# Four raw-weight buffers and five split pairs in place of six and four, with pieces split four ahead

## The chip, the cores and the metric

The kernel runs on one core of one Trainium2 chip. The metric is device time in microseconds (us) of one launch. The engines are named as in the profile: PE is TensorE (PEld its weight loads), DVE is VectorE, ACT is ScalarE, POOL is GpSimd, and SP is SyncE, which here only issues transfers; its queue is written SPq.

## The reference, cut to what matters

One layer of a hybrid decoder block for 256 tokens of width 2048, in float32. Cut down:

```
hn = rms_norm(x, ln_gain)
z  = hn @ w_in + b_in                 # one wide projection, 2048 rows of weights
y_a = rglru(z.lru_x) * silu(z.lru_gate)
y_b = nsa(z.nsa_q, z.k/v ...) * silu(z.nsa_gate)     # compressed, selected, window attention
y_c = fox(z.fox_q, z.fox_k, z.fox_v, z.fox_f) * silu(z.fox_gate)
merged = sum over b of sigmoid(z.merge[b]) * (y[b] @ w_branch[b])
h   = x + merged @ w_out
out = h + sigmoid(h @ w_ple_gate) * rms_norm(p @ w_ple)
```

Nearly all the work is a row of 256 tokens times a great deal of weights, each weight used once.

## The kernel before, in words

**Pieces.** All weights stream through the core once, in the order of their use, as pieces of at most 128 partitions by 1024 float32 (512 KB). There are 384 of them, in the list `halves` that `plan()` makes. A usual piece is two slices of 128 weight rows by 512 columns. Products are made to nearly float32 accuracy out of three cheaper ones: every operand is split into a rounded high part and the remainder, its low part, and PE adds high*high, high*low and low*high (`mm3`). A usual piece is 12 matmuls of 512 columns. In one stretch every fourth piece belongs to the compression of the attention branch (`cmp`); it costs PE only eight short matmuls, though its load and its split are as large as any other.

**The life of a piece.** SP loads it into a buffer `raw` (`issue`). ACT rounds it into the tile `wh`, and DVE subtracts to make `wl` (`cut`). PE then multiplies with both. A load into a raw buffer has to wait until DVE and ACT have read the piece that lay in it; a split into a pair `wh`, `wl` has to wait until PE has finished the piece that lay in that pair. The constants set how many buffers there are and where in the program each step stands:

```
RAW, LOADS, AHEAD = 6, 7, 3
h["raw"] = wp.tile([P, 1024], F32, tag="raw", bufs=RAW, ...)
h["whl"] = [wp.tile([P, 1024], R32, tag=x, bufs=AHEAD + 1, ...) for x in ("wh", "wl")]
for i, h in enumerate(halves):
    while issued <= i + (4 if i < EARLY else LOADS) ...: issue(halves[issued])
    while ready <= i + (2 if i < EARLY else AHEAD) ...: prepare(ready)      # splits the piece
    ... the products of piece i, then side work
```

So, before, the load of piece j waits for the split of piece j-6, and the split of piece j waits for the products of piece j-4. For the first ten pieces (`EARLY`) the program splits only two ahead.

**Side work.** The three mixers, the norms, gates and turns of layout are generators, run a step at a time between pieces by `Side.tick`. Their small products go to four PSUM tiles `bank0` to `bank3`, in between the main products, whose tiles are called `main`. Names that begin with `k_` are side tiles. A turn of layout (`cross`) is a transpose on DVE, four transfers on the SP queue behind whatever loads stand there, and a later read. How much side work goes where is decided while the program is built, by a planner (`Clock`, `Side`) that keeps an estimated time for PE, DVE, ACT and the others: side work stops when DVE or ACT is over a limit ahead of PE (`LIMITS`, 2.5 to 3.5 us), and a small product is put in a margin (`MARGIN`, 1.6 us) after the estimated end of what it reads. The planner knows nothing of the number of buffers. Each engine then runs its own instructions strictly in that order.

Of the kernel before, what the change touches and what calls it, by code (L numbers as in the profile page):

```python
# [1387 lines left out]

RAW, LOADS, AHEAD = 6, 7, 3

FINE = 3
EARLY = 10
# [85 lines left out]
```

## Time and profile before

| | us |
|---|---|
| median of 3 runs | 1060.82 (1060.35 to 1060.99) |
| profiled execution | 1061.77 |
| its span on the core | 1060.0 |
| PE busy | 1053.3 |
| DVE busy | 772.2 |
| ACT busy | 620.6 |

The span runs from the first to the last instruction; the profiled execution's own time is 1.77 us more, which lies around it. Busy PE says little by itself, since matmuls overlap and their ends are modelled. What matters is whether PE waits, and for which engine.

### The profile page before, as it was taken

Reading aid. Unit: us, or ns where it says so; the run is one execution under the profiler, and the core shown is the slowest. Engines: PE = TensorE matmul, PEld = TensorE weight load, DVE = VectorE, ACT = ScalarE, POOL = GpSimd, SP = SyncE. Lnnn points to the kernel's source line nnn. Section 1 sums busy time; section 2 is a strip of 40 time slices with the busy share of each in tenths; the row PEclk is TensorE's granted clock in tenths of the full one; section 3 lists DMA queues with packets and bytes.
Section 4 is the critical chain, followed back from the end, with each engine's and each line's share of the span. In section 5 each row is a group of like instructions: output and inputs, shape, how many; then the busy total and the mean of one; then the engine's idle time right before and its main releaser. Section 6 shows DMA issues by size and latency. Waiting matters only on the chain.

```text
span 1060.0 us, 14061 instructions
## 1 busy us (share of the span) xinstructions
PE 1053.3 (99%) x4903; PEld 879.3 (83%) x4903; DVE 772.2 (73%) x1151; ACT 620.6 (59%) x940; POOL 53.1 (5%) x77
## 2 busy tenths in 40 slices
PE   9999999999999999999999999999999999999998
PEld 7888889888888888888888888888888888888886
DVE  7777889897778678678987965555766566766664
ACT  7668877768766667544645644555555444444442
POOL 0000001110000000020110000000001000000000
PEclk9999999999999999999999999999999999999999
DMA  9767868787657467577677566766676877778751
GB/s 337 248 201 260 257 200 280 233 266 226 217 189 218 150 198 216 182 234 251 194 235 239 186 222 207 223 213 214 219 244 196 264 235 220 236 250 257 278 207 60
DMA packets 86295, 237.52 MB, mean 224 GB/s; under 512 B 14024, under 2 KB 31312, under 8 KB 86224
## 3 DMA queue, kind: packets, MB, share of 16 engines
q1 hardware_dynamic: 81504, 220.87, 64.8%
q0 software_dynamic: 4720, 15.76, 5.5%
q8 instruction: 38, 0.62, 0.3%
q14 instruction: 33, 0.27, 0.1%
HBM read 215.61 MB, written 4.20 MB: 207 GB/s over the span
## 4 chain that ended last, share of the span: by engine, by line
PE 91%; DVE 3%; DMA 2%; ACT 2%; SPq 1%; issue 1%; DVEq 0%; ACTq 0%
PE main L208 87%; PE bank L208 4%; SPq L208 1%; DVE wl L208 1%; DMA raw<-in_w 1%; DMA k_fpz<-k_fprob 1%; DMA k_pz<-k_prob 1%; ACT wh L208 0%; ACT k_pz L208 0%; DVE k_fq L208 0%; DVE k_prob L208 0%; DVE k_fprob L208 0%; DVE k_pt L208 0%; DVE k_fbias L208 0%; DVE k_fx L208 0%
## 5 line engine op out<-in xcount | busy, mean ns | idle before, releaser
L208 DVE TENSOR_TENSOR wl<-raw,wh 128x1024 fp32r<-128x1024 f32 (+2 forms) x388 | 459.8, 1197 | 186.0 <-ACT wh L208 185.2
L208 ACT ACTIVATE wh<-raw 128x1024 fp32r<-128x1024 f32 (+2 forms) x388 | 400.2, 1040 | 318.3 <-PE main L208 281.3
L208 PE MATMUL main<-wh,k_hnh 128*128 128x512 f32 (+2 forms) x1026 | 395.0, 385 | 0.5 <-ACT wh L208 0.5
L208 PE MATMUL main<-wh,k_hnl 128*128 128x512 f32 (+1 forms) x1024 | 393.0, 384 | 0.0
L208 PE MATMUL main<-wl,k_hnh 128*128 128x512 f32 (+2 forms) x1026 | 392.9, 384 | 0.0
L208 PEld LDWEIGHTS main<-wh,k_hnh 128*128 128x128 f32 x1026 | 193.2, 189 | 37.5 <-ACT wh L208 1.1
L208 PEld LDWEIGHTS main<-wh,k_hnl 128*128 128x128 f32 x1024 | 192.5, 188 | 38.1
L208 PEld LDWEIGHTS main<-wl,k_hnh 128*128 128x128 f32 x1026 | 193.2, 189 | 35.9 <-DVE wl L208 0.2
L208 PE MATMUL main<-wl,k_yh 128*128 128x512 f32 x192 | 74.9, 390 | 0.1
L208 PE MATMUL main<-wh,k_yh 128*128 128x512 f32 x192 | 74.9, 390 | 0.0
L208 PE MATMUL main<-wh,k_yl 128*128 128x512 f32 x192 | 74.8, 389 | 0.0
L208 PE MATMUL main<-wh,k_mth 128*128 128x512 f32 x128 | 49.8, 389 | 0.0
L208 PE MATMUL main<-wl,k_mth 128*128 128x512 f32 x128 | 49.8, 389 | 0.0
L208 PE MATMUL main<-wh,k_mtl 128*128 128x512 f32 x128 | 49.8, 389 | 0.0
L208 PE MATMUL main<-wh,k_hth 128*128 128x512 f32 x128 | 49.8, 389 | 0.0
L208 PE MATMUL main<-wl,k_hth 128*128 128x512 f32 x128 | 49.8, 389 | 0.0
L208 PE MATMUL main<-wh,k_htl 128*128 128x512 f32 x128 | 49.8, 389 | 0.0
L208 PEld LDWEIGHTS main<-wl,k_yh 128*128 128x128 f32 x192 | 36.0, 188 | 7.7 <-DVE wl L208 0.5
L208 PEld LDWEIGHTS main<-wh,k_yl 128*128 128x128 f32 x192 | 36.0, 188 | 7.5
L208 PEld LDWEIGHTS main<-wh,k_yh 128*128 128x128 f32 x192 | 36.1, 188 | 7.4
L208 ACT ACTIVATE k_mg<-k_mg 128x512 f32<-128x512 f32 x24 | 15.2, 633 | 26.6 <-DVE k_mg L208 26.3
L208 PEld LDWEIGHTS main<-wl,k_mth 128*128 128x128 f32 x128 | 24.0, 188 | 5.0
(243 smaller groups left out, 948.4 us busy)
## 6 DMA issues: line engine op xcount, KB each, us to landing
raw<-in_w SPq DMA_DIRECT2D x369, 512.0 KB, 4.5
bias<-in_b_in POOLq DMA_DIRECT2D x21, 256.0 KB, 5.2
raw<-in_w SPq DMA_DIRECT2D x8, 408.0 KB, 4.0
k_pz<-k_prob SPq DMA_DIRECT2D x16, 128.0 KB, 4.2
e_dram<-k_e POOLq DMA_DIRECT2D x4, 512.0 KB, 3.6
k_merged<-k_zt SPq DMA_DIRECT2D x16, 128.0 KB, 3.2
k_xc<-in_x POOLq DMA_DIRECT2D x4, 512.0 KB, 6.4
k_hx<-k_zt SPq DMA_DIRECT2D x16, 128.0 KB, 3.6
```

The costliest lines, as they stand in the source:

```text
L208: r = call(out, *args, **kw)
```

## The change

Raw buffers go from six to four, pairs from four to five, and from piece 10 on the program splits a piece four ahead of its products and not three. In memory the two come out alike: 6 + 2*4 = 14 tiles of 4 KB per partition before, and 4 + 2*5 = 14 after.

```
-RAW, LOADS, AHEAD = 6, 7, 3
+RAW, LOADS, AHEAD = 4, 7, 4
```

Now the load of piece j waits for the split of piece j-4, and the split of piece j for the products of piece j-5. Each engine has as many instructions as before (4892 on PE, 1153 on DVE, 869 on ACT, 568 on SP, 82 on POOL); since the planner adds up other times, some stand elsewhere.

On DVE, where the program changes from two ahead to the larger distance: `wl` tiles are low parts of weight pieces, `k_xacc` is the sum of squares for the first norm, `sp_spl` a softplus. Before:

```order
L208 TENSOR_TENSOR wl_425<-raw_366,wh_424 128x1024
L208 TENSOR_TENSOR wl_429<-raw_391,wh_428 128x1024
L208 TENSOR_TENSOR k_xacc_142<-k_xacc_142,k_sq_432 128x512
L208 TENSOR_TENSOR k_xacc_142<-k_xacc_142 128x256
L208 TENSOR_TENSOR wl_451<-raw_416,wh_450 128x1024
L208 TENSOR_SCALAR sp_spl_306<-sp_spl_305 128x8
```

After, in the same place:

```order
L208 TENSOR_TENSOR wl_425<-raw_366,wh_424 128x1024
L208 TENSOR_TENSOR wl_429<-raw_391,wh_428 128x1024
L208 TENSOR_TENSOR wl_433<-raw_416,wh_432 128x1024
L208 TENSOR_TENSOR k_xacc_142<-k_xacc_142,k_sq_436 128x512
L208 TENSOR_TENSOR wl_454<-raw_418,wh_453 128x1024
L208 TENSOR_TENSOR k_xacc_142<-k_xacc_142 128x256
```

The split of the piece in `raw_416` has moved ahead of the side work, and every later split stands one piece further forward.

On the SP queue, where queries are turned (`k_qn`) some 90 pieces in; `raw` rows are loads of pieces. Before:

```order
L208 DMA raw_2197<-in_w 128x1024
L208 DMA raw_2224<-in_w 128x1024
L208 DMA k_qn_2106<-k_zt_2177 128x1x256 x4
L208 DMA raw_2242<-in_w 128x1024
L208 DMA raw_2266<-in_w 128x1024
```

After:

```order
L208 DMA raw_2207<-in_w 128x1024
L208 DMA raw_2228<-in_w 128x1024
L208 DMA raw_2242<-in_w 128x1024
L208 DMA k_qn_2109<-k_zt_2205 128x1x256 x4
L208 DMA raw_2268<-in_w 128x1024
```

The loads stand in the same order, and the turn stands behind one load more. Most turns keep their place.

On PE, the first products of the sparse attention (`bank` from `kk` and the split queries `k_qh`, `k_ql`). Before, they follow main products of the first merged branch (`k_yh`, `k_yl`):

```order
L208 MATMUL main_83<-wl_2939,k_yh_2768 128x512
L208 MATMUL main_83<-wh_2938,k_yl_2769 128x512
L208 MATMUL bank_87<-kk,k_qh_2753 128x272 x2
L208 MATMUL bank_87<-kk,k_ql_2754 128x272
L208 MATMUL bank_88<-kk,k_qh_2753 128x272 x2
```

After, they follow products of the wide projection (`k_hnh`, `k_hnl`):

```order
L208 MATMUL main_84<-wl_2544,k_hnh_128 128x512
L208 MATMUL main_84<-wh_2543,k_hnl_129 128x512
L208 MATMUL bank_87<-kk,k_qh_2623 128x272 x2
L208 MATMUL bank_87<-kk,k_ql_2624 128x272
L208 MATMUL bank_88<-kk,k_qh_2623 128x272 x2
```

The planner has put this group 16 pieces earlier (at piece 103 and not 119). The other groups of that branch come 0 to 6 pieces earlier, the last one where it was, and all groups of the forgetting attention (`fox`, with `k_fk`, `k_fpt`, `k_fx`) stand at the same pieces as before.

## The prediction

> **What bounds the kernel now.** I read the page first, then the waits of PE, the chain that ended last, and the engines by stage.
>
> ```profile
> PE 1053.3 (99%) x4903; PEld 879.3 (83%) x4903; DVE 772.2 (73%) x1151; ACT 620.6 (59%) x940; POOL 53.1 (5%) x77
> ```
>
> Busy PE could hide stalls, so the waits and the pace must confirm it. All waits of PE in the span:
>
> ```profile
> PE bank L208 <- PEq L1473: 0.8, 1, 0.8
> PE main L208 <- ACT wh L208: 0.5, 1, 0.5
> PE bank L208 <- DVE k_fpt L208: 0.2, 1, 0.2
> ```
>
> The chain that ended last (start, length, what, how many):
>
> ```profile
> 5.39 37.24 PE main L208 x158
> ...
> 107.83 0.93 PE bank L208 x8
> 108.77 8.19 PE main L208 x36
> ...
> 617.00 438.03 PE main L208 x1932
> ```
>
> From 617 us to the tail the chain is PE alone, 1932 matmuls at 226.7 ns; the 36 at 108.77 take 227.5 ns each, in the busiest stretch of side work. So PE runs at one pace nearly throughout and sets the time. By stage (window, its length, then busy PE, PEld, DVE, ACT, POOL, granted clock, DMA share, GB/s):
>
> ```profile
> 60.00:250.00 190.00, 190.00 (x1004) 162.40 (x1003) 163.29 (x241) 143.14 (x219) 12.59 (x14) 1.00 0.75 239
> 250.00:617.00 367.00, 366.53 (x1714) 305.64 (x1713) 287.99 (x550) 228.04 (x412) 21.58 (x31) 1.00 0.68 211
> 617.00:1055.00 438.00, 438.00 (x1933) 362.32 (x1931) 276.85 (x282) 208.35 (x245) 16.27 (x24) 1.00 0.70 220
> ```
>
> DVE is 86% busy from 60 to 250 us (163.29 of 190), 78% to 617 and 63% after.
>
> **First term: splits one piece further ahead.** No instruction is added or removed, so PE's work is unchanged. A stall of PE that the earlier split could remove is needed for a gain. The 0.8 us and the 0.5 us lie in the first 6 us, which the change leaves alone (first four loads, two ahead for ten pieces). The middle window shows 367.00 - 366.53 = 0.47 us idle, the others none. Gain between 0 and 0.47; I take 0.3, since the late split at 371 us (below) is one of its causes and gains a piece.
>
> **Second term: the load waits for the split four pieces back.** With six buffers the load waits for the split six back. One such place, DVE, ACT and SP rows of the stretch (piece numbers from counting: DVE's rows from 108.41 are pieces 40, 41 with 42, and 43; ACT's from 116.33 are 44, 45 with 46, and 47):
>
> ```profile
> 108.41 1.22 DVE L208 TENSOR_TENSOR wl<-raw,wh 128x1024 fp32r<-128x1024 f32 x1
> 111.43 2.35 DVE L208 TENSOR_TENSOR wl<-raw,wh 128x1024 fp32r<-128x1024 f32 x2
> 114.37 1.22 DVE L208 TENSOR_TENSOR wl<-raw,wh 128x1024 fp32r<-128x1024 f32 x1
> ...
> 116.33 1.06 ACT L208 ACTIVATE wh<-raw 128x1024 fp32r<-128x1024 f32 x1
> 118.16 2.01 ACT L208 ACTIVATE wh<-raw 128x1024 fp32r<-128x1024 f32 x2
> 120.66 1.06 ACT L208 ACTIVATE wh<-raw 128x1024 fp32r<-128x1024 f32 x1
> ...
> 109.66 0.33 SPq L208 DMA_DIRECT2D raw<-in_w  x1
> ```
>
> Piece 40's split ends at 109.63 and the load of piece 46 leaves at 109.66: SP does wait for it. After the change the load of 44 waits there. All splits shift by a piece together, so the distances in these rows carry over: from the end of split 40 to ACT's start on 44 is 116.33 - 109.63 = 6.7 us, from 43 to 47 it is 120.66 - 115.59 = 5.1. A load needs this long (loads of pieces from 60 to 250 us, then from 617 on):
>
> ```profile
>   PE main L208: 24.7, 19
> DMA to landing us min/median/max: 2.8/4.6/7.2
> ...
>   PE main L208: 185.4, 119
> DMA to landing us min/median/max: 3.5/4.5/8.3
> ```
>
> With the median 4.6 there remain 0.5 to 2.1 us; with the slowest, 7.2, ACT gets its piece 2.1 us late. Today ACT hardly ever waits for a load:
>
> ```profile
> ACT wh L208 <- DMA raw<-in_w: 2.3, 5, 0.9
> ```
>
> What covers a late load: ACT's own idle time for lack of a pair (24.7 us from 60 to 250, in the fence above), DVE's queue behind ACT, and the piece more of lead. How thin the cover was:
>
> ```profile
> 160.53 1.06 ACT L208 ACTIVATE wh<-raw 128x1024 fp32r<-128x1024 f32 x1 [0.60 <-PE main L208]
> 165.06 2.10 DVE L208 TENSOR_TENSOR wl<-raw,wh 128x1024 fp32r<-128x1024 f32 x2
> 166.50 0.93 PE bank L208 x8
> ```
>
> The first of the two low parts at 165.06 is done near 166.2, and PE multiplies with it from 166.5 at the latest; ACT had finished 3.5 us before DVE began, so there ACT may be 3 us late without loss. The new lead gives DVE one piece more: four pieces, one of them `cmp`, take 108.77 + 8.19 - 107.83 = 9.13 us, 2.3 each. So 2.1 late against 2.3 gained: I take 0.3 us of stalls, from 0 up to the first rival's 7. After 617 us PE holds ACT back 119 times for 185.4 us in all, and a late load only uses that up: nothing. Without that cover the price would be the first rival's.
>
> [...]
>
> **Third term: the SP queue and thin joints.** SP runs in order, so turns of layout stand behind loads that now wait for a newer split, at most one piece (2.7 us at 12 matmuls of 227 ns) longer. SP already waits mostly for splits, and three places have nothing to spare:
>
> ```profile
> SPq L208 <- DVE wl L208: 588.5, 276, 8.4
> ```
>
> ```profile
> 370.67 1.19 DVE wl L208
> 371.91 4.15 PE main L208 x17
> ...
> 395.63 1.16 DVE k_prob L208
> 396.84 0.56 SPq L208
> ...
> 398.76 3.35 DMA k_pz<-k_prob
> 402.13 1.07 ACT k_pt L208
> ...
> 405.80 0.63 PE bank L208 x3
> ...
> 538.59 2.02 DMA k_fpz<-k_fprob
> 540.76 0.53 ACT k_fpt L208
> 541.93 0.80 PE bank L208 x4
> ```
>
> At 371 the split itself was last; it gains a piece. At 402 and 540 ACT reads a turn within 0.2 us of its landing, and PE's small products follow. Before the one at 402, DVE finished its transpose at 396.79 and SP issued at 396.84: SP stood free, so much of the 2.7 us need not show. But the attention between 300 and 430 us is also put in another order, first products 16 pieces earlier, which may thin it or crowd it. Bounds -0.5 (the crowding goes) to +5 (two joints fully late); I take 0.5, near the small end, because the forgetting attention keeps its places.
>
> **The first ten pieces.** The load of piece 4 now waits for the split of piece 0 and so on, while the transfers are at their limit (337 GB/s in the first slice), so a later issue lands about as early: 0.
>
> ```profile
> GB/s 337 248 201 260 257 200 280 233 266 226 217 189 218 150 198 216 182 234 251 194 235 239 186 222 207 223 213 214 219 244 196 264 235 220 236 250 257 278 207 60
> ```
>
> **Sum.** -0.3 + 0.3 + 0.5 + 0 = +0.5 us on the profiled span of 1060.0, which with 1.77 around it makes 1061.77, itself 0.95 above the median. On the median 1060.82 this gives 1061.3: no change that a measurement of this kernel tells from none (0.2%, 2.1 us).
>
> **Rivals.**
>
> *The ring of four loads binds (slower).* One turn of a raw buffer is load 4.6, ACT 1.05, DVE 1.2, together 6.9 us, against 9.27 us that PE needs for four pieces from 60 to 250 us (190 us, 82 splits). If waiting in ACT's and DVE's queues takes more than 2.4 us per turn on average, the ring sets the pace. For it: DVE is 86% busy there and the 3.5 us wait at 161.6 is in the rows. Against it: ACT still has 24.7 us to give. At 3.0 us the loss is 0.6 in each of 20 turns, 12 us, less some 5 of lead at the start: +7, 1068 us.
>
> *The turns come late at the thin joints (slower).* Third term at its upper end, two joints at 2 us or more: 1065. For it the zero slack at 402 and 540; against it SP standing free at 396.84, and the forgetting attention's turns at their old places.
>
> *A stall that lets the clock drop.* The launch shows slow matmuls:
>
> ```profile
> 8.11 0.63 PE L208 MATMUL main<-wl,k_hnh 128*128 128x512 f32 x1
> 8.54 0.63 PE L208 MATMUL main<-wh,k_hnl 128*128 128x512 f32 x1
> ```
>
> They start 0.43 us apart, against 0.227 in the chain later, and this lasts from 5.39 to at least 8.54. If one stall brought that back, it would cost itself (the length of such a slow stretch, 3 us or more) and half of a like stretch after it, 1.6: 1061.3 + 3 + 1.6 = 1066. [...]
>
> *The lead pays (faster).* At most 0.47 us of idle PE can go, under the 2.1 that would be told from no change.
>
> **Chances.** Forecast 0.67; ring 0.18; joints 0.10; clock 0.02; over 0.2% faster 0.03. So faster 0.03, same 0.67, slower 0.30. The range reaches from 1059.8 (0.47 gained and half a us of scatter, as the runs had) to 1067, which takes in the joints, the clock and the milder half of the ring.
>
> **What the next profile would show.** If I am right: PE's waits together stay under 3 us, the chain from about 617 us is PE alone; ACT's waits for loads grow from 2.3 us but stay under some 25, mostly before 250 us; SP's waits for low parts grow from 588.5; ACT's waits for PE shrink before 250 us. If the ring binds, PE waits for `wl` or `wh` many times between 60 and 250 us, and ACT for loads just before. If the joints fail, PE waits a few times for `bank` operands between 300 and 620 us. A wait of PE after 617 us would speak against all of this.

## The result, and the profile after

| | before | after |
|---|---|---|
| median (6 runs each, same chip) | 1061.17 us | 1067.58 us (1065.41 to 1069.2) |
| ratio | | 1.0057 [1.0042, 1.0071] |
| span of the profiled execution | 1060.0 us | 1063.6 us |

The change makes the kernel 0.6% slower. The profiled execution is the fastest of the six and lost 3.6 us, while the median lost 6.4. These are two questions: where 3.6 us went, and what most other runs lost besides. One of the ten runs of e5 below took 1164.15 us at a granted clock of 0.851, and the ratios leave such a run out.

The chain that ended last says when it was lost. Its long last piece is as long as before (438.03 us) and starts 3.75 us later, so all of it is lost before 620 us:

```profile
620.75 438.01 PE main L208 x1932
```

Waits of PE after (engine, what waits, for what: us in total, times, longest):

```profile
PE bank L208 <- DVE k_fpt L208: 2.4, 1, 2.4
PE main L208 <- ACT wh L208: 1.1, 1, 1.1
PE bank L208 <- PEq L1473: 0.8, 1, 0.8
PE bank L208 <- DVE k_wds L208: 0.7, 1, 0.7
PE main L208 <- ACT k_yh L208: 0.6, 1, 0.6
...
```

(Two more are of 0.3 and 0.2 us.) The 1.1 us lies at 7 us and does not show on balance: set side by side, the pieces of the two traces start 0.4 us earlier after the change at piece 12. Luck has a part in that, since the full clock is granted from 4.6 us on in this execution and from 9.2 us on in the one before, where matmuls of 512 columns still start 0.43 us apart at 8.54 and 0.23 us apart from 9.33. By 62 us, with some side work moved, 0.1 us of it is left. The pieces start 0.9 us later after 124 us (`k_wds`, gate weights of the recurrent mixer), 1.5 us later by piece 192, and 3.7 us later after 543 us (`k_fpt`, turned probabilities of the forgetting attention). Two places carry most of it: 0.9 us arise at the first and 2.2 us at the second.

ACT's and SP's waits grew as the steps of the change would have it:

```profile
ACT wh L208 <- DMA raw<-in_w: 56.6, 51, 5.4
ACT wh L208 <- PE main L208: 217.8, 146, 2.4
...
SPq L208 <- DVE wl L208: 654.6, 293, 6.6
```

ACT waits for loads 51 times and not 5, and SP stands for low parts 66 us longer. By stage (columns as in the prediction):

```profile
60.00:250.00 190.00, 189.00 (x1000) 161.34 (x999) 161.53 (x238) 139.98 (x216) 12.01 (x13) 1.00 0.72 234
250.00:617.00 367.00, 363.97 (x1701) 303.45 (x1700) 288.18 (x549) 227.76 (x414) 22.72 (x33) 1.00 0.68 210
```

PE is idle 1.00 us in the first stage (before 0) and 3.03 in the second (before 0.47).

**The place at 543 us.** SP's queue there, before and then after (a row is one kind of transfer, and its length runs from the first to the last of the group):

```profile
533.38 0.33 SPq L208 DMA_DIRECT2D raw<-in_w  x1
533.76 2.51 SPq L208 DMA_DIRECT2D k_fq<-k_zt  x4
536.37 2.81 SPq L208 DMA_DIRECT2D k_fpz<-k_fprob  x4
```

```profile
534.89 2.30 SPq L208 DMA_DIRECT2D raw<-in_w  x2
537.25 2.52 SPq L208 DMA_DIRECT2D k_fq<-k_zt  x4
539.87 2.99 SPq L208 DMA_DIRECT2D k_fpz<-k_fprob  x4
```

DVE's low parts after, then ACT and PE behind the turn:

```profile
535.58 3.49 DVE L208 TENSOR_TENSOR wl<-raw,wh 128x1024 fp32r<-128x1024 f32 x3
...
544.46 0.52 ACT L208 ACTIVATE k_fpt<-k_fpz 128x384 fp32r<-128x384 f32 x1 [3.95 <-DMA k_fpz<-k_fprob]
...
545.63 0.80 PE L208 MATMUL bank<-k_fpt,k_fx 128*128 128x512 f32 x4 [2.42 <-DVE k_fpt L208]
```

The first of the three low parts ends near 536.8 (a third of 3.49 behind 535.58). The second of the two loads on SP leaves just then, at 536.9 (537.25 less the 0.33 us that a load takes), and the two turns behind it can't pass it. The second of them leaves at 539.87 and not 536.37, 3.50 us later. Of this, 1.51 us were there already: DVE ended the transpose for it at 532.63 and not 531.12, because all work was that late by then. The other 1.99 us are the longer stand on SP. ACT stands 3.95 us for it, and PE 2.42.

**The place at 124 us** has its root on SP too, 20 us and more earlier. SP, before and then after, where the recurrent mixer's input is turned back (`k_zt<-k_gl`):

```profile
101.81 0.33 SPq L208 DMA_DIRECT2D raw<-in_w  x1
102.19 4.85 SPq L208 DMA_DIRECT2D k_zt<-k_gl  x4
```

```profile
101.78 3.74 SPq L208 DMA_DIRECT2D raw<-in_w  x3
105.57 2.94 SPq L208 DMA_DIRECT2D k_zt<-k_gl  x4
```

And DVE's row before (its transpose for that turn), then its rows after, with the low parts next to it, then ACT's:

```profile
99.43 1.25 DVE L208 STREAM_TRANSPOSE k_gl<-k_zt 128x1024 f32<-128x1024 f32 x1 [0.43 <-ACT k_zt L208]
```

```profile
101.67 1.25 DVE L208 STREAM_TRANSPOSE k_gl<-k_zt 128x1024 f32<-128x1024 f32 x1
102.84 2.32 DVE L208 TENSOR_TENSOR wl<-raw,wh 128x1024 fp32r<-128x1024 f32 x2
...
112.49 1.28 ACT L208 ACT_TABLE_LOAD   x1 [1.31 <-DMA k_zt<-k_gl]
```

The transpose is done at 102.92, but two loads stand ahead of the turn on SP, and they wait for the two low parts that DVE makes after it. The last of these ends at 105.16 and the turn leaves at 105.57, 3.38 us later than before. Only 1.14 us of that is the longer stand at this spot. The transpose itself ends 2.24 us later than before (102.92 and not 100.68), and there an earlier turn has a part: the mixer's input (`k_zt<-k_u`) left SP at 80.30 and not 78.70, and ACT stood 1.05 us for it at 85 us, where it had not waited before. So the delays of successive turns add up. At both places the turn stands behind as many loads on SP as before the change (48 at 102 us, for instance); only what these loads wait for is newer. ACT then runs its chain of gates late, DVE makes `k_wds` late, and PE waits at 124.

### The profile page after: what moved, and what is told of

It is laid out like the page before. It is cut to its first block, busy times and chain, and to the rows that moved or that the text cites. A ratio compares the mean times of both kernels' runs of the same rounds, so it can differ in the third digit from the quotient of the medians.

```text
span 1063.6 us, 14072 instructions
## 1 busy us (share of the span) xinstructions
PE 1052.5 (99%) x4903; PEld 877.6 (83%) x4903; DVE 773.1 (73%) x1151; ACT 618.8 (58%) x940; POOL 53.6 (5%) x77
## 4 chain that ended last, share of the span: by engine, by line
PE 95%; DMA 2%; DVE 1%; SPq 1%; ACT 1%; issue 0%; ACTq 0%; DVEq 0%
PE main L208 91%; PE bank L208 5%; DMA raw<-in_w 1%; SPq L208 1%; DVE wl L208 1%; ACT wh L208 0%; DMA k_fpz<-k_fprob 0%; DVE k_fin L208 0%; ACT k_yh L208 0%; DVE k_yl L208 0%; DVE k_wds L208 0%; DVE k_fpt L208 0%; ACT k_fpt L208 0%; ACT k_hs L208 0%; DVE k_ucs L208 0%
## 5 line engine op out<-in xcount | busy, mean ns | idle before, releaser
L208 ACT ACTIVATE wh<-raw 128x1024 fp32r<-128x1024 f32 (+2 forms) x388 | 401.1, 1040 | 305.6 <-PE main L208 217.8
L208 PEld LDWEIGHTS main<-wh,k_mtl 128*128 128x128 f32 x128 | 24.0, 188 | 5.0
```

Of the source, the lines that this page charges most:

```text
L208: r = call(out, *args, **kw)
```

## The experiments

Two numbers describe every version. In program order, the load of piece i+LOADS stands at step i and waits for the split of piece i+LOADS-RAW, which was written at step i+LOADS-RAW-AHEAD. So a load stands **RAW + AHEAD - LOADS** steps behind the split that it waits for (call it the slack of SP), and it is written **LOADS - AHEAD** pieces ahead of its own split (the lead of the load). The two add up to RAW. Before: slack 2, lead 4. After: slack 1, lead 3.

Theory A: the loss is the slack. SP stands at loads that wait for a newer split, and turns of layout behind them come late. Theory B: the loss is the short ring, loads of pieces reach ACT late. Theory C: it is the planner's other order of the side work.

| run | RAW, LOADS, AHEAD | slack, lead | median us | ratio to before |
|---|---|---|---|---|
| before | 6, 7, 3 | 2, 4 | 1061.17 | |
| after | 4, 7, 4 | 1, 3 | 1067.58 | 1.0057 [1.0042, 1.0071] |
| e5 | 5, 7, 4 | 2, 3 | 1060.78 | 0.9993 [0.9983, 1.0003] |
| e9 | 5, 8, 4 | 1, 4 | 1066.54 | 1.0043 [1.0030, 1.0056] |
| e10 | 4, 7, 4 | 1, 3 | 1068.32 | 1.0060 [1.0048, 1.0073] |
| e3 | 5, 7, 3 | 1, 4 | 1071.25 | 1.0089 [1.0072, 1.0106] |
| e6 | 6, 8, 3 | 1, 5 | 1070.65 | 1.0087 [1.0072, 1.0102] |
| e2 | 4, 7, 3 | 0, 4 | 1091.74 | 1.0280 [1.0264, 1.0297] |
| e7 | 6, 9, 3 | 0, 6 | 1086.08 | 1.0231 [1.0215, 1.0246] |
| e4 | 4, 6, 4 | 2, 2 | 1067.51 | 1.0051 [1.0035, 1.0068] |
| e1 | 4, 5, 4 | 3, 1 | 1077.16 | 1.0137 [1.0116, 1.0159] |
| e8 | 4, 7, 4, a load held at turns | varies | 1067.13 | 1.0052 [1.0034, 1.0070] |

**Loads written later, with four buffers (e1, e4).**

```
-RAW, LOADS, AHEAD = 4, 7, 4
+RAW, LOADS, AHEAD = 4, 5, 4      # e1;  e4: 4, 6, 4
```

> The changed kernel with loads written five pieces ahead in the program and not seven (LOADS 5; four raw buffers, five pairs, splits four ahead as in the change). The buffers, and so the ring of load, split and free buffer, are the same; only the place of a load on the SP queue moves back by two pieces, behind any turn of layout that was written in between. Theory A (turns of layout stand on SP behind loads that wait for a newer split): 1061 to 1063 us, and the 2.4 us wait of PE for k_fpt is gone. Theory B (the ring of four buffers is too short, pieces reach ACT late): 1066 to 1069, as the change. Theory C (the planner's other order of side work): 1066 to 1069.

> As the first of these, with loads six pieces ahead (LOADS 6): one piece of the seven taken back. Theory A: between, 1061 to 1066. Theory B and theory C: 1066 to 1069.

Theory A alone would have e1 near the kernel before. It took 1077.16 instead. But e1 is no clean test: in its trace the planner's order of side work is another again, on DVE and ACT about as far from the change's as that is from the order before. In e4 all three engines keep the change's order. ACT's waits for loads in e1 with one of them, then the same and PE's waits in e4:

```profile
ACT wh L208 <- DMA raw<-in_w: 174.2, 79, 7.8
...
552.55 1.06 ACT L208 ACTIVATE wh<-raw 128x1024 fp32r<-128x1024 f32 x1 [5.23 <-DMA raw<-in_w]
```

```profile
ACT wh L208 <- DMA raw<-in_w: 93.4, 61, 5.8
...
PE main L208 <- ACT wh L208: 1.8, 3, 0.7
...
PE bank L208 <- DVE k_fpt L208: 0.2, 1, 0.2
```

In e1 PE still waits 2.5 us for `k_fpt`, against theory A's sign. The cause is another: its turn has left SP by 548.3, and ACT makes `k_fpt` at 553.82, behind the piece for which it stands 5.23 us. In e4 the wait for `k_fpt` is gone (0.2 us and not 2.4), as A has it for slack 2. But now pieces are late: ACT waits 93.4 us for loads, once for 4.92 us at 114.56, and PE waits for `wh` three times and for `wl` twice (1.0 us). What a ring of four gives back to SP's turns it takes from the loads. So B is real too in these versions; how much of it is in the change, later runs must tell.

**Undoing one half of the change each (e2, e3).**

```
-RAW, LOADS, AHEAD = 4, 7, 4
+RAW, LOADS, AHEAD = 4, 7, 3      # e2: four buffers, splits three ahead;  e3: 5, 7, 3
```

> The change's raw part alone: four raw buffers, but four pairs and splits three ahead as before, so every engine's order is that of before. The load of piece j waits for a split that is written after it in the program. Theory A: worse than the change, 1068 to 1085, since SP stands behind a still newer split. Theory B: worse than the change too, 1068 to 1100, with many waits of PE for wl or wh, since the load has no more than the time of four splits and the lead is one piece less. Theory C: 1061, as before.

> Five raw buffers, four pairs, splits three ahead: the order of before on every engine. On SP a load waits for a split that is written one piece ahead of it in the program, just as in the change; the ring has five buffers. Theory A: 1063 to 1068, most of the change's loss. Theory B: 1061 to 1062. Theory C: 1061.

The instructions of PE, DVE and ACT stand in the same order in both as before the change, so what is lost here is waiting, and the slow clock that follows some waits (0.992 and 0.997 on the mean in the profiled executions; more on this below). Four buffers with the old lead cost 30 us: the splits four ahead are what makes four buffers bearable, since they add a step of slack. One buffer fewer (e3) costs some 9 us with ACT hardly waiting for loads. ACT's rows of e3:

```profile
ACT k_pt L208 <- DMA k_pz<-k_prob: 14.8, 5, 6.2
ACT wh L208 <- DMA raw<-in_w: 6.1, 8, 2.0
```

It waits for turns (`k_pz`, 14.8 us). On SP that turn leaves at 399.83 behind three loads, while before it left at 396.84.

**All buffers, loads written earlier (e6, e7).** If slack is what counts, it can be taken away without touching a buffer:

```
-RAW, LOADS, AHEAD = 6, 7, 3
+RAW, LOADS, AHEAD = 6, 8, 3      # e6;  e7: 6, 9, 3
```

> The kernel before (six raw buffers, four pairs, splits three ahead) with loads written eight pieces ahead: a load waits on SP for a split that is written one piece before it, as in the change, while the ring keeps its six buffers. Theory A alone: 1063 to 1067, with longer waits of ACT for turned tiles and of PE for what follows from them. Theory B alone: 1061.

> As the run above with loads nine pieces ahead: a load waits for a split written after it, as with four raw buffers and splits three ahead (1091.7 us), but with the ring of six. Theory A alone: 1068 to 1090. Theory B alone: 1061 to 1062. Where it lies between 1061 and 1091.7 tells how the loss of that kernel divides.

With six buffers and slack 1 the kernel takes 1070.65 us, as with five and slack 1 (1071.25). With slack 0 it takes 1086.08, against 1091.74 with four buffers and slack 0. In e7 ACT waits for loads 1.6 us in all and for two kinds of turns 39 us; the splits that stand behind these waits in its queue come late as well (PE waits 7.4 us for `wl`):

```profile
ACT k_pt L208 <- DMA k_pz<-k_prob: 24.0, 6, 5.7
ACT k_fpt L208 <- DMA k_fpz<-k_fprob: 15.2, 6, 5.7
ACT wh L208 <- DMA raw<-in_w: 1.6, 3, 1.2
```

So a load that stands too early on SP costs 9 us with one step of slack and 25 with none, though nothing waits for the load itself. Some 5 of e2's 30 us are the ring (ratios 1.0280 and 1.0231).

**The change with a fifth buffer (e5).** Five buffers and five pairs need one more tile; two pools of side tiles give it up:

```
-RAW, LOADS, AHEAD = 4, 7, 4
+RAW, LOADS, AHEAD = 5, 7, 4
-    k2 = pool("k2", 10)
-    k1 = pool("k1", 8)
+    k2 = pool("k2", 9)
+    k1 = pool("k1", 6)
```

> The change with five raw buffers and not four (splits four ahead, five pairs, loads seven ahead, the change's order on every engine); room for the buffer is made by one tile less of 2 KB and two less of 1 KB for side work. Theory A (turns of layout stand on SP behind loads that wait for a new split): the load now waits for a split written two pieces before it, as with six and three: 1061 to 1063 us. Theory B (the ring of four is too short): 1061 to 1063. Theory C (the other order of side work): 1066 to 1068.

1060.78 us, no different from before. All waits of PE in it:

```profile
PE bank L208 <- PEq L1473: 0.8, 1, 0.8
PE main L208 <- DVE wl L208: 0.2, 1, 0.2
PE main L208 <- ACT wh L208: 0.2, 1, 0.2
```

It has the change's lead and, in its trace, the change's order of side work throughout, so theory C falls, and the lead by itself neither costs nor pays. But a fifth buffer adds to slack and ring at once; this run doesn't tell A from B. Two more do.

**Five buffers with slack 1, and the pools alone (e9, e10).**

```
-RAW, LOADS, AHEAD = 5, 7, 4      # e5
+RAW, LOADS, AHEAD = 5, 8, 4      # e9;  e10: 4, 7, 4, with e5's pools
```

> Five raw buffers, a lead of four, and loads written eight ahead; two pools of side tiles are smaller by one and two tiles to make room, as in the version with loads seven ahead, which took 1060.8 us. The only difference to that version is that a load now stands one piece of program behind the split it waits for, and not two. If turns of layout are lost on SP behind such loads, the time is 1066 to 1070 and PE waits for k_fpt or sp_m for 2 us or more in all, with ACT waiting under 15 us for loads of raw pieces. If only the ring of four was too short, the time stays at 1061, since this ring has five.

> The change as it was (four raw buffers, loads seven ahead, lead of four), with the two pools of side tiles smaller by one and two tiles. If the smaller pools had a part in the version that came out at 1060.8, this one is below 1065. If the fifth raw buffer did it, this one is at 1067 to 1068, with the waits of the change: one turn (k_fpt) at 543 us, and ACT waiting 50 us or more for loads.

e9 is 1066.54 and e10 1068.32: the pools had no part in e5, and the change's loss is there without its short ring. PE's waits of e9, and ACT's for loads:

```profile
PE bank L208 <- DVE k_fpt L208: 2.2, 1, 2.2
PE bank L208 <- DVE k_wds L208: 1.3, 1, 1.3
...
ACT wh L208 <- DMA raw<-in_w: 6.7, 10, 2.1
```

They are the change's two places with 6.7 us of waiting for loads in the place of 56.6. SP and ACT of e9 at the first place read like those of after:

```profile
101.95 3.75 SPq L208 DMA_DIRECT2D raw<-in_w  x3
105.75 2.56 SPq L208 DMA_DIRECT2D k_zt<-k_gl  x4
...
113.57 1.28 ACT L208 ACT_TABLE_LOAD   x1 [3.01 <-DMA k_zt<-k_gl]
```

Between e5 and e9 only the slack is smaller (and the lead longer), and the order on PE, DVE and ACT is the same. So theory A holds for the change. What the ring of four adds is e10 minus e9, 1.8 us with overlapping intervals. One part stays open: with slack 1 the transfers of `k_fpz` also take longer once they have left (3.5 us at the median in after and 3.4 in e9, against 2.5 before and 2.1 in e5), and no run here shows why.

**Holding a load back only where a turn waits (e8).** The change, with one load fewer ahead while a turn's transfers are due:

```
+    turning = [0]                   # raised and lowered around the wait in `cross`
-        while issued <= i + (4 if i < EARLY else LOADS) and ...
+        while issued <= i + (4 if i < EARLY else LOADS - (turning[0] > 0)) and ...
```

> The changed kernel, in which one load is held back in the program while a turn of layout waits for its transfers, so that every turn stands ahead of one load more on SP; other loads keep their place. Theory A: 1062 to 1065, without the 2.4 us wait for k_fpt. Theory B: 1066 to 1069, and PE's waits for split pieces or for what ACT makes stay or grow.

1067.13 us. The wait for `k_fpt` is 0.4 us, but ACT waits longer for loads, once 5.62 us at 114 us, just ahead of the gates behind `k_wds`:

```profile
PE bank L208 <- DVE k_wds L208: 1.8, 1, 1.8
...
ACT wh L208 <- DMA raw<-in_w: 76.7, 52, 5.6
```

As with e4, the loss moves from turns to loads. No version with four buffers came back to 1061.

**Stalls of known length (e11, e12).** What is left is the median, 2 us above the profiled execution of after. Its six runs, by mean granted clock: at 1.000 they took 1065.41, 1065.6 and 1067.26 us, at .997 or .998 1067.89, 1068.44 and 1069.2. In some of the profiles above, a stall of PE is followed by matmuls 0.43 us apart, as at the launch. To see what brings that about, DVE repeats some low parts of the kernel before, where PE otherwise never waits:

```
# cut to the lines that matter
+AGAIN = {235: 7, 255: 7, 275: 7, 295: 7, 315: 7, 335: 7}     # e12: 6, 6, 6, 8, 8, 8
             V.tensor_tensor(*args, op=OP.subtract)
+            for _ in range(again):
+                nc.vector.tensor_tensor(*args, op=OP.subtract)
```

> The kernel before, in which DVE writes the low part of six pieces (235, 255, 275, 295, 315, 335, all after 617 us) eight times over and not once, with the same result each time. The planner is not told. Before, DVE ends the low part some 5.9 us before PE needs it (a piece is 2.72 us, the split of a piece starts when the one four back is multiplied, ACT takes 1.06 and DVE 1.22), so seven times 1.22 more makes PE wait about 2.6 us at each of the six places, 15.6 us in all, as long as the change's stall at 543 us. Theory 1, a stall that short costs its own length and nothing else: the granted clock is 1.0 in every window and the time is 1061.5 + 15.6 = 1077. [...]

> As the one with six stalls, with the low parts of pieces 235, 255 and 275 written seven times (a stall of about 1.4 us each) and those of 295, 315 and 335 nine times (about 3.8 us each): again 15.6 us of stalls. Theory 1: 1077 and a clock of 1.0 throughout. [...]

e11 took 1097.51 us and e12 1093.21, both more than the 1077 of theory 1. The stalls came out longer than I had worked out: the gaps between matmuls were 3.0, 3.0, 5.9, 3.1, 4.1 and 4.1 us in e11 (23 in all and not 15.6), and 1.75, 1.75, 4.6, 4.3, 5.4 and 5.4 in e12. So there are no stalls of 2.6 us here. But what follows them is plain. In e12 the first stall, in e11 the first (window, its length, busy PE, ... then granted clock as the third number from the end):

```profile
648.00:651.00 3.00, 1.41 (x6) 0.86 (x5) 2.93 (x4) 1.06 (x1) 0.00 (x0) 1.00 0.00 0
651.00:654.00 3.00, 3.00 (x15) 2.44 (x14) 3.00 (x4) 0.00 (x0) 0.00 (x0) 1.00 0.64 202
```

```profile
651.00:654.00 3.00, 0.39 (x2) 0.00 (x0) 2.93 (x3) 1.06 (x1) 0.00 (x0) 1.00 0.00 0
654.00:657.00 3.00, 2.76 (x9) 2.23 (x10) 3.00 (x4) 0.00 (x0) 0.00 (x0) 0.78 0.58 142
657.00:660.00 3.00, 3.00 (x10) 2.36 (x9) 1.92 (x3) 1.68 (x3) 0.00 (x0) 0.65 0.82 306
```

After 1.75 us the clock stays at 1.0. After 3.0 us it is 0.78 and then 0.65, and there are ten matmuls in 3 us and not some 14. Of the ten stalls of 3 us and more, nine were followed by such a stretch; of the two of 1.75, none. (The tenth is one of 3.1 us in e11; why it was not, nothing here shows.) In e11 the stalls (23.2 us) and the slow matmuls behind them (10.0, their excess over the usual distance added up) make up 33.2 of its 35.1 us above before's span. In the two rows of e11 the clock is short of full by 0.22 and by 0.35 of 3 us, so as an estimate from them a slow stretch costs 1.7 us. Five at 1.7 would be 8.5 of the 10.0, so some were longer. Theory 1 falls.

The same behind the change's own stall at 543 us, e9 (2.2 us for `k_fpt`) and then after (2.4):

```profile
546.00:549.00 3.00, 3.00 (x10) 2.42 (x10) 3.00 (x6) 0.97 (x3) 0.00 (x0) 0.50 0.79 249
```

```profile
546.00:549.00 3.00, 3.00 (x16) 2.53 (x15) 3.00 (x5) 2.29 (x4) 0.00 (x0) 1.00 0.83 283
```

Nearly the same stall: the clock is 0.50 in the one and 1.00 in the other, and nothing here shows what decides it. e9's five runs fall in two groups likewise, 1065.02 and 1065.06 at a mean clock of 1.000, and 1066.54, 1067.03 and 1068.38 at .998. e10, which has the change's three constants and the same stall of 2.4 us, did lose some of its clock there: from 530 to 550 us, where PE is idle for 2.40 us, its mean granted clock is 0.94, and that of after 1.00 (2.42 us idle). That the runs at .997 or .998 of the change itself lost theirs there was not seen, since only its profiled execution left a trace. 1065.4 with one slow stretch of 1.7 us, or two, would be 1067.1 or 1068.8, an estimate.

## Why the prediction was wrong

It forecast 1061.3, with a range to 1067.0; 1067.58 was measured. By its own steps:

- **First term, splits further ahead (-0.3).** Held as far as can be told: e5 has that lead and the new order, and its ratio is 0.9993 [0.9983, 1.0003].
- **Second term, loads wait for the split four back (+0.3).** The waits were undersized, the cover was not. ACT's waits for loads were to stay under 25 us and came to 56.6 (23.3 of them from 60 to 250 us). But ACT's waits for PE fell from 281.3 to 217.8 us, as the term had it, and e9, with nearly none of these late loads, lost as much as the change within 1.8 us. The rival of the ring, though its 1068 is near the number measured, is not what happened: PE waited for a `wl` or `wh` twice in all.
- **Third term, SP queue and thin joints (+0.5, bounds -0.5 to +5).** This is the step that failed, by its size: the mechanism was named and priced at 0.5. It measured 3.2 us at the two places, of 3.6 on the span. The rows for it stood in the prediction: zero slack at 402 and 540, and SP waiting for low parts 588.5 us. From one favourable row (SP stood free at 396.84), and because the forgetting attention keeps its places, I took the small end for all turns; the larger loss is in the forgetting attention, at those places. The joint at 402 did hold, the one at 540 did not, and a third, the turn at 102, I had not looked at, because its late effect shows as `k_wds` 20 us on. The cap of one piece, 2.7 us, held for each stand on SP (1.99 and 1.14 us longer), but it was no cap on how late a turn is: the two left 3.50 and 3.38 us late, since what earlier turns and stalls had lost came on top.
- **The rival of late turns (1065, chance 0.10)** is what the profiled execution shows in mechanism. That the number fits as well (1065.41) is partly luck: one of the rival's two joints held, and the other place was not among them.
- **The rival of the clock (1066, chance 0.02).** Its price was about right, its condition was not. I asked for a stall of 3 us or more, with none in sight; those 3 us were my estimate from the slow stretch at the launch, and no run shows them as a least length. The change's own stall of 2.4 us came with a lower clock in e10 (0.94 from 530 to 550 us), and 2.2 us in e9 with 0.50 behind it. And it was set beside the late turns as another case, while it comes on top of them: 1065.4 and a slow stretch or two at 1.7 us would give 1067.1 to 1068.8, around the measured median.
- **The first ten pieces (0)** held, with luck in it: 0.4 us earlier at piece 12, where PE waited 1.1 us for a piece but had the full clock 4.6 us sooner. That 337 GB/s is a limit no row shows: it is a mean over 26.5 us, and from 10 to 15 us before moved 406 GB/s, with a DMA share of 1.04.

Of the signs named for the next profile, PE alone in the chain after 617 us, no wait of PE after it, and SP's longer waits came. PE's waits came to 6.1 us and not under 3. The sign of the joints, `bank` operands between 300 and 620 us, came once, at 543.

## What to carry to other kernels

Where one in-order queue issues both bulk loads and small urgent transfers, count for each load how many steps of the program lie between it and the event that frees its buffer: here two steps cost nothing, one cost 5 to 9 us, and none 25, though the loads themselves were in time. The buffers of a ring are shared out between that slack and the lead of the load over its use (here 2 + 3 = 5 was the least that ran at full speed), so a ring smaller than that loses at one end or the other, wherever the loads are written; a queue of their own for the urgent transfers was not tried. And price a stall of a busy TensorE at its length, plus some 1.7 us (the estimate from e11) for slow matmuls that may follow: here they did behind 2.2 us in e9, and did not behind 2.4 us in after or 1.75 us in e12.

## What the runs showed of the hardware

Stalls of PE and the clock granted behind them, from the rows shown above:

| run | stall, us | granted clock behind it |
|---|---|---|
| e12, first stall | 1.75 | 1.00 (651 to 654 us) |
| e9 | 2.2 | 0.50 (546 to 549 us) |
| after | 2.4 | 1.00 (546 to 549 us) |
| e11, first stall | 3.0 | 0.78, 0.65 (654 to 660 us) |

In these runs the length of a stall doesn't tell by itself: 2.2 us in e9 came with half clock and 2.4 us in after did not. What else it depends on was not shown. Of e9, the windows on either side have 0.94 (543 to 546 us) and 0.99 (549 to 552); with the 0.50 between them this is again 1.7 us short of full clock.

Nor was the idle time always in one piece: in e4 slow matmuls came behind two waits of 0.72 and 0.76 us (gaps of 0.88 and 1.03 beyond the usual distance). From 123.80 us on eight matmuls run some 0.43 us apart, and the next, from 127.20, 0.23 us apart again. Rows of e4:

```profile
121.24 0.50 PE L208 MATMUL main<-wh,k_hnh 128*128 128x512 f32 x1 [0.72 <-ACT wh L208]
...
122.50 0.50 PE L208 MATMUL main<-wl,k_hnh 128*128 128x512 f32 x1 [0.76 <-DVE wl L208]
...
123.80 0.63 PE L208 MATMUL main<-wh,k_hnh 128*128 128x512 f32 x1
124.23 0.63 PE L208 MATMUL main<-wl,k_hnh 128*128 128x512 f32 x1
...
126.79 0.57 PE L208 MATMUL main<-wl,k_hnh 128*128 128x512 f32 x1
127.20 0.39 PE L208 MATMUL main<-wh,k_hnl 128*128 128x512 f32 x1
127.43 0.40 PE L208 MATMUL main<-wh,k_hnh 128*128 128x512 f32 x1
```
